# Per-token norm factor multiplied into the input once, ahead of the conditioning scale and shift, in a fused hybrid diffusion layer

## The chip, the cores and the metric

The kernel runs on one core of a Trainium2 chip. The metric is device time in microseconds for one execution of the whole layer, the median of several executions; smaller is better.

## The reference

One layer with a batch of 1, 1024 latent tokens of width 1024, and 256 context tokens. The part that the change touches is the first normalisation; cut to it:

```python
mod = (silu(c) @ ada_w + ada_b)          # 6 pieces: sh1, sc1, g1, sh2, sc2, g2
h  = rms_norm(x,   norm1_w) * (1 + sc1)  + sh1
hc = rms_norm(ctx, norm1_w) * (1 + sc1c) + sh1c
p, pc = h @ w_in, hc @ w_in              # q, k, v, z, x, B, C, dt columns
attn  = neighbourhood_attention(rope(q), rope(k), v, context keys and values)
y_ssd = rms_norm(bidirectional_ssd(...) * silu(z))
x = x + g1 * (concat(attn, y_ssd) @ w_out)
x = x + g2 * conv_glu(rms_norm(x, norm2_w) * (1 + sc2) + sh2)
return rms_norm(x, final_norm_w)
```

`rms_norm(x, w)` is x times the inverse root mean square of its row, times w.

## The kernel before

Activations lie with features on the 128 partitions (eight tiles, `kt` 0 to 7) and tokens along the free dimension; the 1024 tokens are taken in two halves, x0 and x1, of 512. A matrix product is done in three products of high and low parts (`mm3`): `hh` and `hl` are the high and low parts of the normalised input, `wh` and `wl` those of a weight, and each `kt` takes hh·wh, hl·wh and hh·wl. `load_w` loads a weight block of 128 columns (`ws`), splits it on ACT (`wh`, L79) and DVE (`wl`, L80). One such block over all 1024 tokens is a "unit" (`fu_...`), 48 matmuls of 128x512 into one PSUM tile of the pool `mmp`, which has three tiles.

The start of the kernel is the norm. `stats` squares the input on ACT and adds on DVE (`sqa_x`, L152), then sums over partitions on PE (`stat_x`). `rstd_rows` makes the inverse norm, a diagonal `dg_x` of it on DVE, and by a matmul with ones (L105) a tile `rbt` in PSUM that holds each token's factor on all partitions; `rbt` is one of the three tiles of `mmp`, and both halves lie in it. `ada(b)` loads a block of `ada_w` (`adaw`), multiplies it with the conditioning (`adap`, 8 matmuls, shown as x16 in some rows), copies it (`adas`) and transposes it (`mp`), from which DVE makes two columns each of `mod` and `modc`. Blocks 4 to 7 hold the scales and 0 to 3 the shifts, so that two tiles `kt` need block 4+i and block i. Then `norm` runs for each half and `kt`: DVE multiplies input, scale and `rbt` into `ny` (L176), ACT adds the shift and rounds to `hh` (L177), DVE takes `hl` as the rest (L178).

Behind the norm come the units of the q, k projections: `fu_qk00`, `fu_qk01`, `fu_qk10`, `fu_qk11`, `fu_qk20` and on. Each pair of units is rotated on DVE: `rp1_00`, `rp1_01` read the first unit's PSUM tile (L297), `rp2_00`, `rp2_01` the second's (L298), and the tiles come free with these. `context` normalises the context tokens: squares `sq_c` on ACT, `sqa_c` adds on DVE, `stat_c` on PE. Between them stands the load of `crow` (L319), a row for the late conditioning, put through Silu on ACT (L320); its place `yz` overlaps memory that the norm's work tiles hold before. In ACT's list, in both kernels, this Silu and the load of its table stand between `sq_c5` and `sq_c6`, so that the last two squares, the splits of the next weights and all that needs them come behind it.

The instruction order of each engine is written at build time by a scheduler that simulates the program; each engine then runs its own list in that order and waits where an operand isn't ready. Tiles of a pool are reused when their last reader is done.

Of the kernel before, what the change touches and what calls it, by code (L numbers as in the profile page):

```python
# [10 lines left out]
FP = mybir.dt.float32  # L11
FR = mybir.dt.float32r
AF = mybir.ActivationFunctionType
OP = mybir.AluOpType
# [3 lines left out]
P = 128  # L18
T = 1024
TC = 256  # L20
KT = 8
# [15 lines left out]
def hymba(ctx: ExitStack, tc: tile.TileContext, A):  # L37
    nc = tc.nc
    act, dve, pool, pe, sp = nc.scalar, nc.vector, nc.gpsimd, nc.tensor, nc.sync
# [4 lines left out]
    def f32(ap):  # L44
        return ap.bitcast(FP)
# [6 lines left out]
    mod = const.tile([P, 48], FP, name="mod")  # L52
    modc = const.tile([P, 16], FP, name="modc")
    scl = const.tile([P, 3, KT], FP, name="scl")
# [20 lines left out]
    def load_w(src, nk, nf, name):  # L75
        n = nk * nf
        s, h, l = (w_tile(tag, f"{tag}_{name}") for tag in ("ws", "wh", "wl"))
        sp.dma_start(s[:, :n], src)
        split[0] = act.activation(h[:, :n], s[:, :n], AF.Copy).ins  # L79
        dve.tensor_tensor(l[:, :n], s[:, :n], f32(h[:, :n]), OP.subtract)  # L80
        pat = "p (k f) -> p k f"
        return h[:, :n].rearrange(pat, k=nk), l[:, :n].rearrange(pat, k=nk)
# [10 lines left out]
    def rstd_rows(ps_pool, wk, sums, n, tag, key, dtag, dg=None, rb=None):  # L93
        st = wk.tile([P, 8], FP, tag="r_st", name=f"rst_{key}")
        act.activation(st[:, :n], sums, AF.Sqrt, bias=epst, scale=1.0 / 1024)
        dve.reciprocal(st[:, :n], st[:, :n])
        if rb is None:
            rb = ps_pool.tile([P, n * P], FP, tag=tag, name=f"rb_{key}")
        if dg is None:
            dg = wk.tile([P, n, P], FP, tag=dtag, name=f"dg_{key}", bufs=1)  # L100
        dve.tensor_tensor(dg, ident[:, None, :].to_broadcast([P, n, P]),
                          st[:, :n][:, :, None].to_broadcast([P, n, P]), OP.mult)
        for t in range(0, n, 4):
            e = min(n, t + 4)
            pe.matmul(rb[:, t * P:e * P], ones, dg[:, t:e], start=True, stop=True)  # L105
        return rb
# [1 line left out]

    pa = ExitStack()
    hx = pa.enter_context(tc.tile_pool(name="hx", reuse_waits="tile", bufs=1))  # L110
    pc = ExitStack()
    hxc = pc.enter_context(tc.tile_pool(name="hxc", reuse_waits="tile", bufs=1))
    hh = hx.tile([P, KT, T], FR, name="hh")
    hl = hx.tile([P, KT, T], FR, name="hl")
    ch = hxc.tile([P, KT, TC], FR, name="ch")
    cl = hxc.tile([P, KT, TC], FR, name="cl")

    mmp = pa.enter_context(tc.tile_pool(name="mmp", reuse_waits="tile", bufs=3, space=PSUM))
    m1p = pa.enter_context(tc.tile_pool(name="m1p", reuse_waits="tile", bufs=2, space=PSUM))
    pre = {}  # L120

    with ExitStack() as p0:
        adap = p0.enter_context(tc.tile_pool(name="adap", reuse_waits="tile", bufs=4))
        xin = p0.enter_context(tc.tile_pool(name="xin", reuse_waits="tile", bufs=1))
        wk0 = p0.enter_context(tc.tile_pool(name="wk0", reuse_waits="tile", bufs=2))

        cc = wk0.tile([P, KT, 2], FP, name="cc", bufs=1)
        sc = hx.tile([P, KT, 32], FP, name="sc")
        sel = wk0.tile([P, 2], FP, name="sel", bufs=1)
        xt = xin.tile([P, KT, T], FP, name="xt")  # L130
        sp.dma_start(cc, A["cc"])
        xh = [xt[:, :, 512 * h:512 * h + 512] for h in range(2)]

        def load_x(h):
            for kt in range(0, KT, 2):
                sp.dma_start(xh[h][:, kt:kt + 2], A["xt"][:, kt:kt + 2, 512 * h:512 * h + 512])

        load_x(0)
        sp.dma_start(sel, A["sel"])
        sp.dma_start(vec, A["vec"])  # L140
        sp.dma_start(cst, A["cst"])
        dve.memset(sc, 0.0)
        act.activation(sc[:, :, 0:2], cc, AF.Silu)

        def stats(wk0, src, n, key):
            st = m1p.tile([P, 8], FP, tag="m1", name=f"stat_{key}")
            acc = wk0.tile([P, n * P], FP, tag=f"sqa{n}", name=f"sqa_{key}", bufs=1)
            for kt in range(KT):
                sq = acc if kt == 0 else wk0.tile([P, n * P], FP, tag=f"ny{n}", name=f"sq_{key}{kt}", bufs=n)
                act.activation(sq, src[:, kt], AF.Square)  # L150
                if kt:
                    dve.tensor_tensor(acc, acc, sq, OP.add)  # L152
            for t in range(n):
                pe.matmul(st[:, t:t + 1], acc[:, t * P:(t + 1) * P], ones1, start=True, stop=True)
            return st[:, :n]

        def ada(b):
            w = adap.tile([P, KT, 256], FP, tag="ada", name=f"adaw{b}")
            sp.dma_start(w, A["ada_w"][b])
            pr = m1p.tile([P, 256], FP, tag="m1", name=f"adap{b}")  # L160
            for kt in range(KT):
                j = kt % 4
                pe.matmul(pr[32 * j:32 * j + 32], sc[:, kt], w[:, kt], start=kt < 4, stop=kt >= 4,
                          skip_group_check=True)
            sb = wk0.tile([P, 256], FP, tag="adas", name=f"adas{b}")
            act.activation(sb, pr, AF.Copy)
            mp = m1p.tile([P, 2, 2], FP, tag="m1", name=f"mp{b}")
            for f in range(2):
                pe.matmul(mp[:, f], sb[:, f * P:(f + 1) * P], sel, start=True, stop=True)
            c0 = 2 * b  # L170
            for m_, col in ((mod, 0), (modc, 1)):
                dve.tensor_tensor(m_[:, c0:c0 + 2], mp[:, :, col], vec[:, V_AB + c0:V_AB + c0 + 2], OP.add)

        def norm(src, rb, a, b, oh, ol, kt, n, key):
            y = wk0.tile([P, n], FP, tag=f"ny{n // P}", name=f"ny_{key}{kt}", bufs=n // P)
            dve.scalar_tensor_tensor(y, src[:, kt], a, rb, OP.mult, OP.mult)  # L176
            act.activation(oh[:, kt], y, AF.Identity, bias=b)  # L177
            dve.scalar_tensor_tensor(ol[:, kt], y, b, f32(oh[:, kt]), OP.add, OP.subtract)  # L178

        rbt = mmp.tile([P, T], FP, tag="mm", name="rbt")  # L180
        rbx = [rbt[:, 512 * h:512 * h + 512] for h in range(2)]
        rstd_rows(mmp, wk0, stats(wk0, xh[0], 4, "x0"), 4, "mm", "x0", "sqa4", rb=rbx[0])
        for i in range(4):
            ada(4 + i)
            if i == 0:
                load_x(1)
            ada(i)
            if i < 3:
                pre[i] = load_w(A["wf"][8 + i], KT, P, f"qk0{i}")
            s2 = slice(2 * i, 2 * i + 2)  # L190
            for j, m_ in enumerate((mod, modc)):
                dve.scalar_tensor_tensor(scl[:, j, s2], m_[:, 8 + 2 * i:10 + 2 * i], 1.0,
                                         vec[:, V_N1 + 2 * i:V_N1 + 2 * i + 2], OP.add, OP.mult)
            for h in range(2):
                if i == 0 and h:
                    rstd_rows(mmp, wk0, stats(wk0, xh[1], 4, "x1"), 4, "mm", "x1", "sqa4", rb=rbx[1])
                for kt in (2 * i, 2 * i + 1):
                    c = slice(512 * h, 512 * h + 512)
                    norm(xh[h], rbx[h], scl[:, 0, kt:kt + 1], mod[:, kt:kt + 1], hh[:, :, c], hl[:, :, c], kt, 512, f"x{h}")

    hs = (hh, hl)
    cs = (ch, cl)
    dtr = hx.tile([P, 10, 16], FP, name="dtr")
# [38 lines left out]
    with ExitStack() as p1:  # L242
# [67 lines left out]
        for b in range(2):  # L310
# [12 lines left out]
            for cb in range(4):  # L323
                win = v_d[4 * cb:4 * cb + 4, :, fs].rearrange("g (i r c) f -> r c (g i) f", i=2, r=2)
                for r in range(2):
                    p0 = 64 * r + CB0[cb]
# [273 lines left out]
    for i in range(2):  # L600
        t = at.tile([P, 1024], FP, name=f"tabt{i}", bufs=1)
# [474 lines left out]
    for hf_ in range(2):  # L1076
        c = slice(512 * hf_, 512 * hf_ + 512)
# [156 lines left out]
```

## Time and profile before

| what | value |
|---|---|
| median of 3 runs | 1395.33 us (1395.41, 1390.05, 1395.33) |
| profiled execution | 1391.19 us, span 1389.4 us |
| PE busy | 1328.5 us, 96% |
| DVE busy | 855.1 us, 62% |
| ACT busy | 628.0 us, 45% |
| POOL busy | 308.0 us, 22% |
| mean granted TensorE clock | 0.989 |

PE is TensorE's matmuls, DVE is VectorE, ACT is ScalarE, POOL is GpSimd, and SP is the engine whose queue issues most loads. The span is the time from the first to the last instruction. An engine that is busy 96% of the span sets the time nearly everywhere; the profile's rows say where it doesn't.

### The profile page before, as it was taken

The numbers are of one execution on the slowest core, as the hardware profiler recorded it, in microseconds if no ns is written. First come the engines' busy times: TensorE is split into PE (matmuls) and PEld (weight loads), VectorE is DVE, ScalarE is ACT, GpSimd is POOL, SyncE is SP. The second block draws the span as 40 slices with busy tenths as digits, with TensorE's granted clock in tenths as the row PEclk, the third lists the DMA queues.
The fourth block names the chain that finished last, engine by engine and source line by source line (L and its number), as shares of the span: only waits on it lengthen the run. The fifth ranks groups of instructions, "written<-read, shape, count | busy, mean of one in ns | idle before, by whom it ended". The sixth has DMA issues, their size and how long they took to land.

```text
span 1389.4 us, 20030 instructions
## 1 busy us (share of the span) xinstructions
PE 1328.5 (96%) x7539; PEld 1116.4 (80%) x7539; DVE 855.1 (62%) x1343; ACT 628.0 (45%) x1052; POOL 308.0 (22%) x297
## 2 busy tenths in 40 slices
PE   5999999999989999999999999999999999999996
PEld 3788998889968877777887888888888878888884
DVE  5683347652367766647887555666556586585663
ACT  5441224342155557536556444454445464364440
POOL 0000000013667862000222222221222111201210
PEclk9999999999999999999999999999999999999998
DMA  9565575621697697333858576766677796777771
GB/s 370 212 159 139 142 231 198 220 92 38 164 269 213 206 241 250 124 114 121 205 121 212 153 185 163 175 153 157 144 174 169 204 289 184 169 214 210 182 187 71
DMA packets 118160, 251.02 MB, mean 181 GB/s; under 512 B 11944, under 2 KB 37288, under 8 KB 116784
## 3 DMA queue, kind: packets, MB, share of 16 engines
q1 hardware_dynamic: 92576, 197.58, 44.4%
q0 software_dynamic: 25488, 52.18, 20.2%
q8 instruction: 59, 0.97, 0.3%
q14 instruction: 37, 0.30, 0.1%
HBM read 212.16 MB, written 37.55 MB: 180 GB/s over the span
## 4 chain that ended last, share of the span: by engine, by line
PE 79%; DMA 8%; DVE 4%; ACT 4%; issue 2%; POOL 1%; SPq 0%; DVEq 0%; POOLq 0%; ACTq 0%
PE u L872 28%; PE fu_qk L90 7%; PE fu_x L90 6%; PE pd L90 6%; PE tu_v L90 4%; PE tu_z L90 3%; PE oc L90 3%; PE av L666 3%; PE pm L1044 2%; PE pt L648 2%; PE os L90 2%; PE s L627 1%; PE oa L90 1%; PE fu_c L90 1%; DMA g_d<-xa 1%
## 5 line engine op out<-in xcount | busy, mean ns | idle before, releaser
L872 PE MATMUL u<-op,whu 128*128 128x512 f32 (+1 forms) x760 | 225.9, 380 | 2.3 <-DVE op L827 0.9
L872 PEld LDWEIGHTS u<-op,whu 128*128 128x128 f32 x760 | 138.9, 188 | 33.3 <-DVE op L827 1.1
L864 ACT ACTIVATE whu<-as 128x512 fp32r<-128x512 f32 x115 | 67.8, 627 | 175.3 <-PE u L872 167.0
L845 POOL DMA_DIRECT2D as<-in_w_up x69 | 66.4, 985 | 360.0 <-DMA as<-in_w_up 153.2
L872 PE MATMUL u<-op,wlu 128*128 128x512 f32 (+1 forms) x380 | 143.4, 378 | 0.0
L872 PE MATMUL u<-opx,whu 128*128 128x512 f32 (+1 forms) x384 | 110.0, 377 | 1.6 <-ACT whu L864 1.2
L865 DVE TENSOR_TENSOR wlu<-as,whu 128x512 fp32r<-128x512 f32 x115 | 76.0, 686 | 25.3 <-ACT whu L864 25.1
L872 PEld LDWEIGHTS u<-opx,whu 128*128 128x128 f32 x384 | 69.8, 188 | 17.2 <-ACT whu L864 2.3
L872 PEld LDWEIGHTS u<-op,wlu 128*128 128x128 f32 x380 | 71.3, 188 | 14.9
L90 PE MATMUL pd<-opx,wh_dn 128*128 128x512 f32 x256 | 81.7, 402 | 0.5 <-ACT wh_dn L79 0.3
L895 DVE TENSOR_TENSOR xa<-u,yz 128x512 f32<-128x512 f32 (+1 forms) x24 | 15.5, 646 | 99.2 <-PE u L872 99.2
L872 PE MATMUL u<-opx,wlu 128*128 128x512 f32 (+1 forms) x192 | 71.7, 376 | 0.0
L639 ACT ACTIVATE pr<-pr,mx 128x640 f32<-128x640 f32 x64 | 52.9, 827 | 39.1 <-DVE mx L638 39.0
L638 DVE CUSTOM_DVE_ANT_0 pr<-s,tabt 128x640 f32<-128x640 f32 x64 | 52.0, 818 | 20.0 <-PE s L628 15.9
L666 PE MATMUL av<-pts,vp 128*64 128x128 f32 x640 | 55.3, 284 | 5.7 <-ACT pts L650 5.2
L852 POOL DMA_DIRECT2D yz<-in_w_up x46 | 55.0, 1230 | 22.8 <-ACT yz L851 21.9
L90 PEld LDWEIGHTS pd<-opx,wh_dn 128*128 128x128 f32 x256 | 47.8, 189 | 12.6 <-ACT wh_dn L79 1.1
L650 ACT ACTIVATE pts<-pt 128x640 f32<-128x640 f32 x64 | 43.9, 696 | 30.3 <-PE pt L648 19.8
L872 PE MATMUL u<-opz,whu 128*128 128x512 f32 (+1 forms) x192 | 56.3, 376 | 0.4 <-ACT yz L887 0.4
L648 PE MATMUL pt<-cst,pr 128*128 128x128 f32 x320 | 48.5, 282 | 6.9 <-ACT pr L639 3.4
L666 PEld LDWEIGHTS av<-pts,vp 128*64 128x64 f32 x640 | 40.5, 139 | 18.2 <-ACT pts L650 8.4
L90 PE MATMUL pd<-opx,wl_dn 128*128 128x512 f32 x128 | 51.2, 402 | 1.6 <-DVE wl_dn L80 1.6
(643 smaller groups left out, 3573.3 us busy)
## 6 DMA issues: line engine op xcount, KB each, us to landing
as<-in_w_up SPq DMA_DIRECT2D x69, 256.0 KB, 4.0
as<-in_w_up POOLq DMA_DIRECT2D x69, 256.0 KB, 3.8
yz<-in_ada_wt SPq DMA_DIRECT2D x32, 512.0 KB, 4.7
ws_dn<-in_w_down SPq DMA_DIRECT2D x32, 448.0 KB, 4.0
as<-in_w_up SPq DMA_DIRECT2D x23, 512.0 KB, 5.5
yz<-in_w_up POOLq DMA_DIRECT2D x46, 256.0 KB, 5.8
g_d<-xa POOLq DMA_DIRECT2D x22, 512.0 KB, 5.0
tabt<-in_tab SPq DMA_DIRECT2D x48, 192.0 KB, 4.4
```

The lines of the kernel that those rows point to most:

```text
L90: pe.matmul(out[:, t0:t1], st(a, k), mv(b, k, t0, t1), start=k == 0 and p == 0, stop=k == kend - 1 and p == 2, **kw)
L638: dve.tensor_tensor_reduce(pr, ps[:, lo:lo + 640], tabt[m % 2][:, 384 * j:384 * j + 640], -1.0, BIG, OP.add, OP.min, mx)
L639: act.activation(pr, pr, AF.Exp, bias=mx, scale=-1.0, accum_out=sm[:, n % 8:n % 8 + 1])
L648: pe.transpose(pt[:, i * P:(i + 1) * P], pr[:, i * P:(i + 1) * P], ident)
L650: act.activation(pts, pt[:, 0:640], AF.Copy)
L666: pe.matmul(av[64 * j:64 * j + 64, cb], vt, pp[j][:, i * P:(i + 1) * P], start=i == 0, stop=i == 4, skip_group_check=True)
L845: pool.dma_start(t, d, accum_op=OP.add)
L852: pool.dma_start(t, d, accum_op=OP.add)
L864: act.activation(h, src, AF.Copy)
L865: dve.tensor_tensor(l, src, f32(h), OP.subtract)
L872: mm = pe.matmul(ps[:, t0:t1], aops[n, o][a][:, k], bops[o][b][:, k, t0:t1], start=first and o < 5 and (t0 == 0 or n == 2), stop=end, skip ...
L1044: pe.matmul(dst[o], aops[n, o][a][:, k], sops[o][b][:, k], start=k == i == 0 and (o in (0, 2, 4) or o > 4 and first), stop=k == 3 and i == ...
```

## The change

The product with `rbt` is taken out of `norm` and done for all eight tiles of a half right after that half's `rbt` (`unit`, in place in the input `xt`). `norm` then has ACT make `hh` from the input with the scale and the shift, ACT take the shift from it again (`nt`, a new tile, with the negated shift `neg`), and DVE make `hl` as input times scale minus `nt`. The pool of `adaw` has six buffers instead of four, and the context's tiles `ch` and `cl` are opened after the norm's pools are closed.

```diff
@@ -108,19 +108,15 @@
 
     pa = ExitStack()
     hx = pa.enter_context(tc.tile_pool(name="hx", reuse_waits="tile", bufs=1))
-    pc = ExitStack()
-    hxc = pc.enter_context(tc.tile_pool(name="hxc", reuse_waits="tile", bufs=1))
     hh = hx.tile([P, KT, T], FR, name="hh")
     hl = hx.tile([P, KT, T], FR, name="hl")
-    ch = hxc.tile([P, KT, TC], FR, name="ch")
-    cl = hxc.tile([P, KT, TC], FR, name="cl")
 
     mmp = pa.enter_context(tc.tile_pool(name="mmp", reuse_waits="tile", bufs=3, space=PSUM))
     m1p = pa.enter_context(tc.tile_pool(name="m1p", reuse_waits="tile", bufs=2, space=PSUM))
     pre = {}
 
     with ExitStack() as p0:
-        adap = p0.enter_context(tc.tile_pool(name="adap", reuse_waits="tile", bufs=4))
+        adap = p0.enter_context(tc.tile_pool(name="adap", reuse_waits="tile", bufs=6))
         xin = p0.enter_context(tc.tile_pool(name="xin", reuse_waits="tile", bufs=1))
         wk0 = p0.enter_context(tc.tile_pool(name="wk0", reuse_waits="tile", bufs=2))
 
@@ -171,15 +167,22 @@
             for m_, col in ((mod, 0), (modc, 1)):
                 dve.tensor_tensor(m_[:, c0:c0 + 2], mp[:, :, col], vec[:, V_AB + c0:V_AB + c0 + 2], OP.add)
 
-        def norm(src, rb, a, b, oh, ol, kt, n, key):
-            y = wk0.tile([P, n], FP, tag=f"ny{n // P}", name=f"ny_{key}{kt}", bufs=n // P)
-            dve.scalar_tensor_tensor(y, src[:, kt], a, rb, OP.mult, OP.mult)
-            act.activation(oh[:, kt], y, AF.Identity, bias=b)
-            dve.scalar_tensor_tensor(ol[:, kt], y, b, f32(oh[:, kt]), OP.add, OP.subtract)
+        neg = wk0.tile([P, KT], FP, name="neg", bufs=1)
+
+        def unit(src, rb):
+            for kt in range(KT):
+                dve.tensor_tensor(src[:, kt], src[:, kt], rb, OP.mult)
+
+        def norm(y, a, b, nb, oh, ol, kt, key):
+            t = wk0.tile([P, 512], FP, tag="nt", name=f"nt_{key}{kt}", bufs=4)
+            act.activation(oh[:, kt], y[:, kt], AF.Identity, scale=a, bias=b)
+            act.activation(t, f32(oh[:, kt]), AF.Identity, bias=nb)
+            dve.scalar_tensor_tensor(ol[:, kt], y[:, kt], a, t, OP.mult, OP.subtract)
 
         rbt = mmp.tile([P, T], FP, tag="mm", name="rbt")
         rbx = [rbt[:, 512 * h:512 * h + 512] for h in range(2)]
         rstd_rows(mmp, wk0, stats(wk0, xh[0], 4, "x0"), 4, "mm", "x0", "sqa4", rb=rbx[0])
+        unit(xh[0], rbx[0])
         for i in range(4):
             ada(4 + i)
             if i == 0:
@@ -191,13 +194,19 @@
             for j, m_ in enumerate((mod, modc)):
                 dve.scalar_tensor_tensor(scl[:, j, s2], m_[:, 8 + 2 * i:10 + 2 * i], 1.0,
                                          vec[:, V_N1 + 2 * i:V_N1 + 2 * i + 2], OP.add, OP.mult)
+            dve.tensor_scalar(neg[:, s2], mod[:, s2], -1.0, None, OP.mult)
             for h in range(2):
                 if i == 0 and h:
                     rstd_rows(mmp, wk0, stats(wk0, xh[1], 4, "x1"), 4, "mm", "x1", "sqa4", rb=rbx[1])
+                    unit(xh[1], rbx[1])
                 for kt in (2 * i, 2 * i + 1):
                     c = slice(512 * h, 512 * h + 512)
-                    norm(xh[h], rbx[h], scl[:, 0, kt:kt + 1], mod[:, kt:kt + 1], hh[:, :, c], hl[:, :, c], kt, 512, f"x{h}")
-
+                    norm(xh[h], scl[:, 0, kt:kt + 1], mod[:, kt:kt + 1], neg[:, kt:kt + 1], hh[:, :, c], hl[:, :, c], kt, f"x{h}")
+
+    pc = ExitStack()
+    hxc = pc.enter_context(tc.tile_pool(name="hxc", reuse_waits="tile", bufs=1))
+    ch = hxc.tile([P, KT, TC], FR, name="ch")
+    cl = hxc.tile([P, KT, TC], FR, name="cl")
     hs = (hh, hl)
     cs = (ch, cl)
     dtr = hx.tile([P, 10, 16], FP, name="dtr")
```

The first place is the start of DVE's list, behind `dg_x0`, the diagonal of the first half's factors; `xt` is the input, `sqa_x1` the sum of squares of the second half. Before:

```order
L101 TENSOR_TENSOR dg_x0_152<-cst_61,rst_x0_149 128x512
L172 TENSOR_TENSOR mod_65<-mp4_168,vec_60 128x2
L172 TENSOR_TENSOR modc_66<-mp4_168,vec_60 128x2
L192 SCALAR_TENSOR_TENSOR scl_67<-mod_65,vec_60 128x2
L192 SCALAR_TENSOR_TENSOR scl_67<-modc_66,vec_60 128x2
L176 SCALAR_TENSOR_TENSOR ny_x00_203<-xt_109,scl_67,rbt_120 128x512
L176 SCALAR_TENSOR_TENSOR ny_x01_207<-xt_109,scl_67,rbt_120 128x512
L152 TENSOR_TENSOR sqa_x1_212<-sqa_x1_212,sq_x11_214 128x512
```

After:

```order
L101 TENSOR_TENSOR dg_x0_148<-cst_61,rst_x0_145 128x512
L174 TENSOR_TENSOR xt_104<-xt_104,rbt_116 128x512 x8
L168 TENSOR_TENSOR mod_65<-mp4_172,vec_60 128x2
L168 TENSOR_TENSOR modc_66<-mp4_172,vec_60 128x2
L148 TENSOR_TENSOR sqa_x1_217<-sqa_x1_217,sq_x11_219 128x512
L195 SCALAR_TENSOR_TENSOR scl_67<-mod_65,vec_60 128x2
L195 SCALAR_TENSOR_TENSOR scl_67<-modc_66,vec_60 128x2
L148 TENSOR_TENSOR sqa_x1_217<-sqa_x1_217,sq_x12_222 128x512
```

Eight products stand ahead of the second half's sums, where two stood, and the later `ny` are gone from the list.

The second place is PE's list just behind the second half's `rbt`, where the first units begin; numbers behind the names are the program's own. Before:

```order
L90 MATMUL fu_qk00_448<-hh_87,wh_qk00_196 128x512
L90 MATMUL fu_qk00_448<-hl_88,wh_qk00_196 128x512
L90 MATMUL fu_qk01_497<-hh_87,wh_qk01_290 128x512
L90 MATMUL fu_qk01_497<-hl_88,wh_qk01_290 128x512
L169 MATMUL mp1_284<-sel_108,adas1_282 128x2 x2
L163 MATMUL adap6_315<-adaw6_313,sc_107 32x256 x8
L90 MATMUL fu_qk00_448<-hl_88,wh_qk00_196 128x512
```

After:

```order
L90 MATMUL fu_qk00_469<-hh_84,wh_qk00_200 128x512
L90 MATMUL fu_qk00_469<-hl_85,wh_qk00_200 128x512
L90 MATMUL fu_qk01_518<-hh_84,wh_qk01_303 128x512
L90 MATMUL fu_qk01_518<-hl_85,wh_qk01_303 128x512
L165 MATMUL mp1_297<-sel_103,adas1_295 128x2 x2
L90 MATMUL fu_qk10_590<-hh_84,wh_qk02_364 128x512 x2
L90 MATMUL fu_qk10_590<-hl_85,wh_qk02_364 128x512
L159 MATMUL adap6_329<-adaw6_327,sc_102 32x256 x8
```

The third unit, `fu_qk10`, which before began behind `mp3_404`, some 55 rows further on, begins here; its PSUM tile is the one that `rbt` held, and it waits for the last product of `unit(x1)`.

The third place is the end of the first three units on PE, and on DVE the rotation that frees their tiles. PE before:

```order
L90 MATMUL fu_qk10_569<-hh_87,wh_qk02_350 128x512 x2
L90 MATMUL fu_qk10_569<-hl_88,wh_qk02_350 128x512 x2
L90 MATMUL fu_qk10_569<-hh_87,wl_qk02_351 128x512 x2
L90 MATMUL fu_qk11_624<-hh_87,wh_qk11_619 128x512 x2
L90 MATMUL fu_qk11_624<-hl_88,wh_qk11_619 128x512 x2
L154 MATMUL stat_c_696<-ones1_63,sqa_c_697 128x1
L90 MATMUL fu_qk11_624<-hh_87,wl_qk11_620 128x512 x2
```

PE after:

```order
L90 MATMUL fu_qk10_590<-hl_85,wh_qk02_364 128x512
L90 MATMUL fu_qk10_590<-hh_84,wl_qk02_365 128x512 x2
L90 MATMUL fu_qk11_645<-hh_84,wh_qk11_640 128x512 x2
L90 MATMUL fu_qk11_645<-hl_85,wh_qk11_640 128x512 x2
L150 MATMUL stat_c_717<-ones1_63,sqa_c_718 128x1 x2
L90 MATMUL fu_qk20_789<-hh_84,wh_qk20_784 128x512 x2
L90 MATMUL fu_qk20_789<-hl_85,wh_qk20_784 128x512 x2
L90 MATMUL fu_qk11_645<-hh_84,wl_qk11_641 128x512 x2
```

On PE all three units now end together, and behind them stand `fu_qk11` and `fu_qk20`, four matmuls each, ahead of the first use of `wl_qk11`. DVE before:

```order
L152 TENSOR_TENSOR sqa_c_697<-sqa_c_697,sq_c5_711 128x256
L152 TENSOR_TENSOR sqa_c_697<-sqa_c_697,sq_c6_714 128x256
L152 TENSOR_TENSOR sqa_c_697<-sqa_c_697,sq_c7_717 128x256
L297 SCALAR_TENSOR_TENSOR rp1_00_547<-fu_qk00_448,cossin_443 128x1024
L297 SCALAR_TENSOR_TENSOR rp1_01_551<-fu_qk00_448,cossin_443 128x1024
L80 TENSOR_TENSOR wl_qk11_620<-ws_qk11_618,wh_qk11_619 128x1024
```

DVE after:

```order
L148 TENSOR_TENSOR sqa_c_718<-sqa_c_718,sq_c5_732 128x256
L148 TENSOR_TENSOR sqa_c_718<-sqa_c_718,sq_c6_735 128x256
L306 SCALAR_TENSOR_TENSOR rp1_00_568<-fu_qk00_469,cossin_464 128x1024
L306 SCALAR_TENSOR_TENSOR rp1_01_572<-fu_qk00_469,cossin_464 128x1024
L148 TENSOR_TENSOR sqa_c_718<-sqa_c_718,sq_c7_738 128x256
L307 SCALAR_TENSOR_TENSOR rp2_00_569<-fu_qk01_518,cossin_464 128x1024
L307 SCALAR_TENSOR_TENSOR rp2_01_573<-fu_qk01_518,cossin_464 128x1024
L80 TENSOR_TENSOR wl_qk11_641<-ws_qk11_639,wh_qk11_640 128x1024
```

On DVE the first two rotations now stand ahead of the last `sqa_c`, and all four ahead of `wl_qk11`. `fu_qk11` takes the PSUM tile that `rp1_01` frees, `fu_qk20` the one that `rp2_01` frees.

## Rows read from the trace of the kernel before

**Rows 1.** Page: head, busy time by engine, GB/s in 40 slices.

```profile
span 1389.4 us, 20030 instructions
...
PE 1328.5 (96%) x7539; PEld 1116.4 (80%) x7539; DVE 855.1 (62%) x1343; ACT 628.0 (45%) x1052; POOL 308.0 (22%) x297
...
GB/s 370 212 159 139 142 231 198 220 92 38 164 269 213 206 241 250 124 114 121 205 121 212 153 185 163 175 153 157 144 174 169 204 289 184 169 214 210 182 187 71
```

**Rows 2.** Timeline of PE, 10 to 39 us: start, length, instruction, idle before.

```profile
15.34 2.08 PE L105 MATMUL rbt<-dg_x,cst 128*128 128x512 f32 x2
...
26.50 1.84 PE L154 MATMUL stat_x<-ones,sqa_x 128*128 128x1 f32 x8 [0.15 <-DVE sqa_x L152]
```

**Rows 3.** Timeline of DVE, 10 to 39 us.

```profile
18.49 1.41 DVE L176 SCALAR_TENSOR_TENSOR ny_x<-xt,scl,rbt 128x512 f32<-128x512 f32 x2
19.81 4.67 DVE L152 TENSOR_TENSOR sqa_x<-sqa_x,sq_x 128x512 f32<-128x512 f32 x6
24.53 1.23 DVE L80 TENSOR_TENSOR wl_qk<-ws_qk,wh_qk 128x1024 fp32r<-128x1024 f32 x1
25.67 0.68 DVE L152 TENSOR_TENSOR sqa_x<-sqa_x,sq_x 128x512 f32<-128x512 f32 x1
```

**Rows 4.** Chain that ended last, 30 to 80 us: start, length, what.

```profile
30.93 1.71 PE rbt L105 x2
...
37.56 1.00 PE adap L163 x16
38.56 4.38 PE fu_qk L90 x18
...
59.19 17.72 PE fu_qk L90 x76
```

**Rows 5.** Timeline of ACT, 55 to 90 us.

```profile
59.42 2.57 ACT L177 ACTIVATE hh<-ny_x,mod 128x512 fp32r<-128x512 f32 x4 [4.43 <-DVE mod L172]
...
67.17 1.28 ACT L320 ACT_TABLE_LOAD   x1 [2.40 <-DMA yz<-in_crow]
```

**Rows 6.** Timeline of DVE, 55 to 90 us.

```profile
60.18 2.75 DVE L178 SCALAR_TENSOR_TENSOR hl<-ny_x,mod,hh 128x512 fp32r<-128x512 f32 x4 [0.73 <-ACT hh L177]
...
69.87 0.96 DVE L152 TENSOR_TENSOR sqa_c<-sqa_c,sq_c 128x256 f32<-128x256 f32 x2 [4.49 <-ACT sq_c L150]
70.74 2.35 DVE L297 SCALAR_TENSOR_TENSOR rp<-fu_qk,cossin 128x1024 f32<-128x1024 f32 x2
73.00 1.22 DVE L80 TENSOR_TENSOR wl_qk<-ws_qk,wh_qk 128x1024 fp32r<-128x1024 f32 x1
```

**Rows 7.** Timeline of SP, 55 to 90 us: the issue of the loads.

```profile
62.99 0.33 SPq L319 DMA_DIRECT2D yz<-in_crow  x1
```

**Rows 8.** Waits of SP's queue, 55 to 75 us: total, times, longest.

```profile
SPq L319 <- DVE hl L178: 8.1, 1, 8.1
```

**Rows 9.** Five stretches: busy PE, PEld, DVE, ACT, POOL; clock, DMA share, GB/s.

```profile
100.00:350.00 250.00, 250.00 (x1575) 225.65 (x1574) 116.74 (x171) 77.50 (x109) 27.34 (x25) 1.00 0.50 152
350.00:560.00 210.00, 193.56 (x1542) 167.65 (x1540) 136.40 (x240) 112.06 (x214) 128.30 (x88) 0.97 0.78 224
490.00:498.00 8.00, 8.00 (x46) 7.09 (x45) 3.41 (x6) 3.86 (x8) 4.40 (x3) 0.57 0.96 206
1100.00:1250.00 150.00, 143.54 (x764) 121.18 (x763) 113.66 (x215) 80.67 (x156) 18.80 (x22) 0.99 0.77 217
1206.00:1212.00 6.00, 5.93 (x29) 5.43 (x30) 5.12 (x9) 3.23 (x6) 1.43 (x2) 0.72 0.76 148
```

**Rows 10.** Timeline of PE, 484 to 492 us.

```profile
489.23 0.43 PE L666 MATMUL av<-pts,vp 128*64 128x128 f32 x2 [2.72 <-ACT pts L650]
```

**Rows 11.** Timeline of PE, 1200 to 1210 us.

```profile
1206.07 0.50 PE L1044 MATMUL pm<-op,whu('d', 0, 2)2_10050 128*128 128x256 f32 x2 [2.08 <-ACT yz L1052]
```

**Rows 12.** Chain that ended last, 370 to 390 us.

```profile
373.60 0.61 ACT zs L570
...
380.66 4.27 DMA tabt<-in_tab
```

## The prediction

> **What bounds the kernel now.** I read the page first: PE is busy 1328.5 of 1389.4 us [rows 1], so the time is PE's work plus the places where PE waits. An edit to DVE and ACT alone counts where it makes PE wait, or stops it from waiting. Next the chain that ended last: behind the second half's `rbt` it is PE alone, 18 matmuls in 4.38 us and so on up to 76 in 17.72 us from 59.19 [rows 4], 0.233 us each, with no wait. So whatever delays PE's start with the second half's factors comes out at the far end of the units, and is not made good in between. Then the timelines of DVE, ACT and SP around the norm. They show what lies just under PE: the last `hl` ends at 60.18 + 2.75 = 62.93 and the load of `crow`, which had waited 8.1 us for it, is issued at 62.99 [rows 6 to 8]. ACT then stands 2.40 us for that load and starts the table at 67.17 [rows 5], DVE gets its last `sqa_c` at 69.87 after 4.49 us of idling, and the two rotations that free a PSUM tile end at 70.74 + 2.35 = 73.09 [rows 6]. PE needs this tile at 59.19 + 72 x 0.233 = 75.98 (the 76 of that row less the four of the fourth unit). The slack is 2.9 us.
>
> **The change, step by step.** Starting at one state for both kernels, I follow the delay.
>
> (1) *Work.* 16 `ny` become 16 unit products, 16 `hl` stay, 4 tiny `neg` come. ACT gets 16 `nt` beside 16 `hh`. Neither engine is the bound (62% and 45%), so this is free where other work covers it; what counts is order.
>
> (2) *First half.* `rbt` x0 ends at 15.34 + 2.08 = 17.42 [rows 2]. An `ny`, one PSUM and one SBUF operand of 128x512, takes 0.70 us (1.41 for two), an add of two SBUF tiles 0.68 to 0.69 [rows 3]. I take 0.70 for a unit product: eight take 5.6 us and end at 23.05, where the two `ny` ended at 19.90. The seven adds, `wl` (1.23 [rows 3]) and the small ones behind them follow; the last add ends near 30.15 against 25.67 + 0.68 = 26.35 before: **+3.8**. The nearest lower bound is half of that price, as for an operation that took two elements a cycle; no row shows such a one on DVE here.
>
> (3) *Second half.* From the start of `stat_x` to the end of `rbt` x1 PE and DVE need 30.93 + 1.71 - 26.50 = 6.14 us [rows 2, 4]; with the delay that ends near 36.35. In the old order PE went on with the blocks of the conditioning and the first two units while two `ny` were made. In the new one the third unit stands there, six matmuls into the first two; its PSUM tile is that of `rbt`, so it waits for all eight products: 36.35 + 5.6 and the start of an instruction, **42.1**. Before, PE was at the same matmul at 38.56, and had one block of `adap` more behind it (1.00 us at 37.56 [rows 4]); so PE is 42.1 + 1.0 - 38.56 = **4.5** late here. I don't see that the work that PE finds meanwhile (a block, six matmuls) shortens it, since it is in both.
>
> (4) *The three units.* Until their end 138 matmuls, 4 blocks and 4 small `mp` follow: 138 x 0.233 + 4.0 + 1.4 = 37.6, with 0.6 for the wait for the last `hl` behind `mp3`, so 80.3 against 75.98: **+4.3**, as it should be from step 3.
>
> (5) *The last shift.* `mp3` now has two thirds of the third unit ahead of it. It ends at 42.1 + 90 x 0.233 + 4.0 + 1.4 = 68.45 against 59.19: +9.3. Behind it `hh` takes 2.57 us for four [rows 5], then four `nt` at the same pitch of 0.64, and `hl`, at 2.75 for four [rows 6], can follow them one by one: the last `hl` ends 6.2 us behind `mp3` (3.74 before) at 74.7. `crow` goes with it. From its issue to the end of the two rotations it was 73.09 - 62.99 = 10.1 us [rows 6, 7], less the 0.4 of the last add, which now stands behind the rotations: PE gets the tile of the fourth unit at **84.4**. It ran dry at 80.3. So the slack of 2.9 us has become a wait of **4.1**: 2.9 are eaten by the delay of `mp3`, `nt` and the rest that PE's own delay doesn't cover. An estimate with the Trainium skill, ScalarE: Activation LUTs, What ACT_TABLE_LOAD costs, goes 0.4 us further: it adds 93 ns for each pointer operand of an ACTIVATE, and the new `hh` has two where L177 has one. No row here shows that pair in this size, and the sum leaves it out.
>
> (6) *Behind it.* Four matmuls on, the fifth unit waits for the other pair of rotations, 84.4 + 0.4 + 2.35 = 87.15, and the next matmul of the fourth for `wl_qk11`, 1.22 us [rows 6] later, **88.35**. PE will by then have done 8 matmuls and `stat_c` of the next work (2.0 us), which before stood at 77.97. So PE is 10.4 late: 4.3 of step 4, 4.1 of step 5, 2.0 here.
>
> (7) *The clock.* The trace shows what PE pays after idling: 2.72 us without a matmul [rows 10], then a mean granted clock of 0.57 over 8 us, which is 0.43 x 8 = 3.4 us of work lost; after 2.08 us [rows 11] it is 0.72 over 6 us, 1.7 lost [rows 9]. That is the lower level of 1.2 GHz for part of these stretches. By the Trainium skill, TensorE: Matmul & The Clock Gate, Part 1, this lower level is the resting state that activity lifts, so that every pause that is long enough costs, that of step 3 too; the rows agree for the two pauses that they show, and by the rule the sum would be up to 1.7 higher, 14.6. Two waits of 4.1 and 2 us with one us of work between them should cost as much again: I take **2.5**, between the two. At step 3 the idle is 1 to 3 us and I take nothing, with 1.7 as its upper bound.
>
> (8) *The rest.* Six buffers let two blocks of `ada_w` overtake the third weight block, 2.1 MB or 5.7 us at the 370 GB/s of the first slice [rows 1]; that weight is needed only at 42.1, so it costs nothing. Its loads end well before that as far as the rate tells (some 12 MB in all by then, 33 us); if the units could start 9 us sooner, it would begin to count. `ch` and `cl` are written long after, by `context`. From 100 to 350 us PE is busy 250.00 of 250.00 [rows 9], in one order in both kernels. At 373.60 the next wait of PE hangs on `zs`, which ACT makes of PE's last result, and the table loads that end the wait are issued behind that (4.27 us from 380.66 [rows 12]). So it moves along with PE and gives nothing back.
>
> The sum is 10.4 + 2.5 = **+12.9**, made against the profiled execution: 1391.2 + 12.9 = 1404.1. That execution lies 4.1 below the median, as one of three runs does; on the median's basis it is 1408.2. I say **1406**, between them. Bounds: with products at half price the second half is ready while PE still works; what then stays is the place of the third unit ahead of `mp3` (24 matmuls, 5.6 us), the `nt` and the dry end: mp3 near 63.9, last `hl` 70.1, fourth unit 79.8, step 6 at 83.7, or +5.7, 1397 to 1401. Upwards the clock of both waits at 3.4 and 1.7 gives +15.5, 1407 to 1411.
>
> **Rivals.**
>
> *A. The attention stage takes it up (not slower).* Over 350 to 560 us PE is busy 193.56 of 210 [rows 9]: 16.4 us of idling with DMA at 0.78, and at 0.96 in 490 to 498. If loads there were the limit and went out at a time that PE doesn't set, the whole 12.9 would vanish: 1391 to 1396. It decides at the table loads: it needs them issued before PE's last `tu_z`. Against it: [rows 12] has their issue behind `zs`. 0.12.
>
> *B. The products are cheap, or run in gaps.* +5.7 as above, 1397 to 1401, mostly within 0.5%. It decides where eight products take under some 2.8 us. The two rows nearest to it are both at 0.7. 0.10.
>
> *C. The reordered down projection gains.* PE's list differs again there, and over 1100 to 1250 us PE idles 6.5 us [rows 9]. If the new order filled these, 12.9 - 6.5 = +6.4: 1397.5 to 1402. The work is the same and its releasers (a weight split, a copy from ACT) aren't touched, so it could as well lose some. 0.12.
>
> *D. The dry end costs more.* If PE stays at the lower level through both waits, or the load of `crow` meets the late blocks, add 3 to 6: 1409 to 1414. 0.08.
>
> *E. The change removes a wait that I don't see* in PE's first 38 us, by earlier blocks of `ada_w`, and is faster, below 1388. For it: PE idles most there. Against it: what ends it is DVE's sums, which come later. 0.05.
>
> The forecast itself holds 0.53, from 1401 to 1410. 0.5%, 7 us, is about what a measurement of this kernel can tell from no change; its three runs spread by 5.4. Slower by more than that: most of the forecast, all of D, a little of C: 0.60. Within it: A in the main, B, C and the lower part of the forecast: 0.32. Faster: E and the edge of A, 0.08. The range of 8 in 10 takes in B, C and most of D: 1394 to 1412. The forecast's own range is 1401 to 1410.
>
> **What would show it.** In the changed kernel's trace: eight products of 0.70 each and the last add near 30; PE standing until 42 for the third unit; `mp3` near 68.5 and the last `hl` near 74.7; the load of `crow` issued right behind; PE idle near 80.3 to 84.4 with DVE's rotations as the releaser, a second wait to 88.4, and a clock below 1 behind them; then the same spacing as before from 90 to 370. I would be wrong if the crow load came out ahead of the last `hl`, if the third unit didn't wait for the eighth product, or if the attention stage began less late than the q, k units ended.

## The result, and the profile after

The changed kernel takes 1407.26 us (median of 4 runs, 1405.49 to 1413.87) against 1395.37 beside it; the ratio is 1.0097, 95% interval [1.0069, 1.0124]. The profiled execution took 1407.97 us. It is slower, by about the forecast amount. The page's head and busy times, to be read beside [rows 1]:

```profile
span 1406.2 us, 20046 instructions
...
PE 1332.6 (95%) x7539; PEld 1117.4 (79%) x7539; DVE 857.0 (61%) x1347; ACT 637.5 (45%) x1068; POOL 312.7 (22%) x297
```

PE has 4 us more of busy time and 17 us more of span: it waits, and works at the lower clock. The timeline of DVE at the start, as [rows 3] (start, length, instruction, idle before):

```profile
17.60 4.87 DVE L174 TENSOR_TENSOR xt<-xt,rbt 128x512 f32<-128x512 f32 x8 [2.61 <-PE rbt L105]
...
28.11 0.69 DVE L148 TENSOR_TENSOR sqa_x<-sqa_x,sq_x 128x512 f32<-128x512 f32 x1
...
35.12 4.87 DVE L174 TENSOR_TENSOR xt<-xt,rbt 128x512 f32<-128x512 f32 x8 [1.83 <-PE rbt L105]
39.91 0.15 DVE L168 TENSOR_TENSOR mod<-mp,vec 128x2 f32<-128x2 f32 x1
```

Eight products take 4.87 us, 0.61 each and not the 0.70 of the forecast. The last sum of the second half ends at 28.80 (26.35 before, 30.15 forecast). The second eight end at 39.99, and behind them stand `mod` and `modc` of the next block. PE's timeline there:

```profile
38.91 0.61 PE L165 MATMUL mp<-sel,adas 128*128 128x2 f32 x4 [1.00 <-ACT adas L162]
40.14 0.70 PE L90 MATMUL fu_qk<-hh,wh_qk 128*128 128x512 f32 x2 [0.62 <-DVE modc L168]
```

PE starts the third unit at 40.14 (42.1 forecast). Its list waits there for the eighth product, which ended 0.15 us before; the trace names `modc`, the last to end on DVE. Two pieces of the chain that ended last (start, length, what), the second half's `rbt` and `mp3`:

```profile
33.38 1.72 PE rbt L105 x2
...
67.13 0.35 PE mp L165 x4
```

`mp3` is done at 67.48 (68.45 forecast, 59.19 before [rows 4]). Then ACT, DVE and SP, as [rows 5 to 7]:

```profile
67.70 2.94 ACT L178 ACTIVATE hh<-xt,mod,scl 128x512 fp32r<-128x512 f32 x4 [5.22 <-DVE mod L168]
70.54 2.55 ACT L179 ACTIVATE nt_x<-hh,neg 128x512 f32<-128x512 f32 x4
...
78.46 1.28 ACT L329 ACT_TABLE_LOAD   x1 [1.71 <-DMA yz<-in_crow]
```

```profile
71.28 2.74 DVE L180 SCALAR_TENSOR_TENSOR hl<-xt,scl,nt_x 128x512 fp32r<-128x512 f32 x4 [3.41 <-ACT nt_x L179]
...
81.50 2.35 DVE L306 SCALAR_TENSOR_TENSOR rp<-fu_qk,cossin 128x1024 f32<-128x1024 f32 x2
...
86.36 3.49 DVE L80 TENSOR_TENSOR wl_qk<-ws_qk,wh_qk 128x1024 fp32r<-128x1024 f32 x3
```

```profile
74.09 0.33 SPq L328 DMA_DIRECT2D yz<-in_crow  x1
```

The last `hl` ends at 74.02, `crow` is issued at 74.09, ACT stands 1.71 us for it, and the two rotations end at 83.85. PE's timeline at that place, and six stretches of 2 us (busy time of PE, PEld, DVE, ACT, POOL; clock, DMA share, GB/s):

```profile
79.34 0.62 PE L90 MATMUL fu_qk<-hh,wl_qk 128*128 128x512 f32 x2
83.99 1.19 PE L90 MATMUL fu_qk<-hh,wh_qk 128*128 128x512 f32 x2 [4.03 <-DVE rp L306]
...
86.59 1.19 PE L90 MATMUL fu_qk<-hh,wh_qk 128*128 128x512 f32 x2
...
90.06 0.62 PE L90 MATMUL fu_qk<-hl,wh_qk 128*128 128x512 f32 x2
```

```profile
80.00:82.00 2.00, 0.00 (x0) 0.00 (x0) 0.85 (x2) 2.00 (x4) 0.00 (x0) 1.00 0.68 279
82.00:84.00 2.00, 0.01 (x1) 0.04 (x1) 2.00 (x3) 2.00 (x3) 0.00 (x0) 0.78 0.00 0
84.00:86.00 2.00, 2.00 (x6) 1.61 (x6) 2.00 (x3) 1.55 (x2) 0.00 (x0) 0.50 0.00 0
86.00:88.00 2.00, 2.00 (x8) 1.72 (x7) 2.00 (x3) 0.26 (x1) 0.00 (x0) 0.50 0.03 8
88.00:90.00 2.00, 2.00 (x6) 1.60 (x5) 2.00 (x3) 0.00 (x0) 0.00 (x0) 0.51 0.72 213
90.00:92.00 2.00, 2.00 (x10) 1.60 (x10) 2.00 (x3) 0.98 (x2) 0.00 (x0) 1.00 0.97 279
```

PE runs dry at 83.99 - 4.03 = 79.96 (80.3 forecast) and goes on at 83.99 (84.4). Behind this the granted clock is 0.50, 1.2 GHz, until 90. The second wait of the forecast does not appear: at the lower clock the eight matmuls and `stat_c` last so long that the second pair of rotations is done when PE comes to `fu_qk20` at 86.59, and `wl_qk11` soon enough too. I call the wait from 79.96 to 83.99 the dry end below.

To follow the lag through the program I counted PE's 7539 matmuls and set the start of the same number in two traces side by side. Behind the units PE's lists are the same in before and after, but for numbers 4404 to 4452 (near 720 us), until 6225; from there to 6892, in the down projection (1135 to 1262 us), they differ in pieces. The table also has the experiments below; a lag is the time by which a kernel is behind the first execution of before.

```
lag to the kernel before, us, at the start of matmul number
                                  300    2000    6200    6500    7500
before (start, us)              70.26  349.60 1128.89 1184.51 1368.95
before, second execution        -1.27   -1.27   +0.67   +0.79   +1.01
changed                         +3.96  +11.04  +11.95  +16.09  +16.64
changed, second execution       +4.38  +11.79  +11.78  +16.10  +16.81
four buffers                    +4.05   +5.82  +12.64  +14.66  +17.00
third unit late                 +4.05   +4.24   +9.05   +9.51  +11.26
crow late                       +4.07   +7.97  +10.80  +10.54  +13.45
third unit and crow late        +3.07   +3.12   +7.38   +5.70   +5.79
second half's products twice    +6.20  +12.71  +17.52  +18.43  +18.41
split only                      +2.18   +2.26   +4.33   +8.47  +13.98
products held                   -1.78   -1.74   -4.47   -5.00   -1.76
products held, again            -0.48   -0.44   +0.70   +1.10   +4.99
products held, four buffers     +7.11   +7.14  +18.95  +23.45  +23.96
```

So 11.0 of the 16.8 us between the two spans arise in the first 92 us, stay to 0.05 us until the attention stage (10.99 at matmul 400), and 4.7 more arise in the down projection. Between them, from 2000 to 6200, lie the attention stage and what follows it, where executions of one kernel drift apart by up to 4 us (the two of the held products). Most experiments lose 2 to 5 us there, the two with four buffers 6.8 and 11.8; why was not looked into. The traces of four buffers, third unit late, split only and held with four buffers are of the slowest execution of their kernel, so their last columns lie above their medians, and the head, up to 2000, is the safest comparison.

### The profile page after: what moved, and what is told of

Read it like the earlier page. It is cut to its first block, busy times and chain, and to the rows that moved or that the text cites. A ratio compares the mean times of both kernels' runs of the same rounds, so it can differ in the third digit from the quotient of the medians.

```text
span 1406.2 us, 20046 instructions
## 1 busy us (share of the span) xinstructions
PE 1332.6 (95%) x7539; PEld 1117.4 (79%) x7539; DVE 857.0 (61%) x1347; ACT 637.5 (45%) x1068; POOL 312.7 (22%) x297
## 4 chain that ended last, share of the span: by engine, by line
PE 71%; DMA 11%; DVE 7%; ACT 4%; issue 3%; POOL 3%; SPq 0%; DVEq 0%; POOLq 0%; ACTq 0%
PE u L881 27%; PE fu_x L90 6%; PE fu_qk L90 6%; PE pd L90 5%; PE tu_v L90 4%; PE oc L90 3%; PE tu_z L90 2%; PE av L675 2%; PE os L90 2%; PE pt L657 2%; DMA seg<-cum_d 2%; PE oa L90 1%; PE fu_c L90 1%; PE s L636 1%; DMA as('d', 1, 2)1_11212<-in_w_down 1%
```

## The experiments

My theory was the forecast's: the place of the products delays PE's start, draws the third unit ahead of `mp3`, so that `crow` and with it ACT's and DVE's queues come late, and PE runs dry. The rivals were the longer split over ACT, the buffers and loads, and a delay that later stages take up. Each ratio is to runs of before on the same chip.

**Controls.** Both kernels again, unchanged.

> The kernel before, unchanged, in a second profiled execution. It tells apart what of the 16.8 us between the two spans (1406.2 and 1389.4) belongs to the change. Theory: the first 360 us repeat to 0.2 us (the 2000th matmul at 349.6), and the 4 to 6 us of difference that arise past 1140 us, in the down projection, are partly the execution's own spread, since the medians differ by 11.9 only: the 7500th matmul at 1369 to 1374. Rival: the reordered down projection costs 5 us in every execution; then it repeats at 1369 within 1 us.

> The changed kernel, unchanged, in a second profiled execution, for the 5 us that it loses past 1140 us in the down projection. Theory from the control of before (whose lag stayed within 1 us there): the reordered list costs 3 to 6 us there in every execution, so the lag between the 6200th and the 7500th matmul grows by 3 to 6 us again. Rival (an accident of one execution): by less than 1.5 us. The first 360 us: 11 us behind within 1.5 us.

Before: 1392.32 us, ratio 0.9982 [0.9964, 0.9999], so the comparison itself can be off by 0.2%. Its head came 1.27 us sooner, where I had expected a repeat within 0.2. Changed: 1409.24, ratio 1.0112 [1.0085, 1.0139]. Its loss in the down projection came again (11.78 to 16.81), before's lag grew by 0.3 there: the theory for it held, an accident is out. PE's waits in the changed kernel's first execution from 1137 us on (engine, line, releaser: total, times, longest):

```profile
PE pd L90 <- DVE wl_dn L80: 2.7, 5, 0.9
PE pd L90 <- ACT op L964: 2.3, 1, 2.3
...
PE pd L90 <- ACT wh_dn L79: 1.5, 3, 0.8
```

These three come to 6.5 us (8.5 in its second execution); the same releasers gave 3.7 in before (1.8, 1.6 and 0.3). They are splits of `w_down` and a copy, in the same code but in another order. That this order costs is shown by the other kernels: two more have the changed kernel's order there, split only and held with four buffers, and the rest have before's. From 6200 to 6500 the four executions with the new order lose 4.1 to 4.5 us, the eight with the old one -1.7 to +2.0. Which move in it does was not tried. From 6500 to 7500 the two groups overlap: 0.5 to 5.5 us and 0 to 3.9.

**Four buffers.**

```diff
-        adap = ...tile_pool(name="adap", reuse_waits="tile", bufs=6)
+        adap = ...tile_pool(name="adap", reuse_waits="tile", bufs=4)
```

> The changed kernel with four buffers for the conditioning blocks instead of six. The prediction's step 8 says that the buffers cost nothing: then the 2000th matmul stays 11 us behind that of before and the time at about 1407. Rival: the two more buffers push the work tiles of the norm onto the place of crow, so that crow's load waits for the last hl; with four its load and its Silu stand in the middle of the norm, the dry end of PE (4.0 us) and the half clock behind it (3.4 us) go, and the 2000th matmul is 3 to 6 us behind: 1399 to 1402.

1400.97 us, ratio 1.0035 [1.0010, 1.0060], and a lag of 5.82 instead of 11.04 at matmul 2000. The rival held, and step 8 fell in that part. In the down projection this kernel has before's order, so its time lacks that loss too. ACT's timeline in this kernel:

```profile
33.00 1.28 ACT L329 ACT_TABLE_LOAD   x1
34.29 1.06 ACT L329 ACTIVATE yz<-yz 128x1024 f32<-128x1024 f32 x1
```

Table and Silu of `crow` stand at 33.0, not behind the last `hl`: the load no longer waits for the norm's tiles. In before, with four buffers too, it does wait for the last `hl` [rows 8], so what frees the place is four buffers together with the late `ch` and `cl`; by the sizes in the code these two take as much as two buffers. PE still waits for the rotations, but 1.1 us instead of 4.0.

**Third unit late.** Its matmuls queued on PE behind `mp3`.

```diff
+            mp3[0] = mpi.ins
 ...
+                with tc.issue_after(mp3[0]) if (blk, f2) == (1, 0) else nullcontext():
                     pq.append(fm_unit(wt, hs, T, mmp, "mm", f"qk{blk}{f2}"))
```

> The changed kernel with the third unit queued on PE behind mp3, as before, so that it no longer waits early for the eighth product nor delays mp3. Theory: mp3 and with it the last hl and crow come some 7 us sooner (mp3 near 61 to 62), the dry end of 4.0 us and its half clock go; what stays is the start of the first two units 2 to 4 us late. 2000th matmul 3 to 5 us behind before, time 1399 to 1401. Rival (the loss is the longer chain hh, nt, hl or the early loads): the dry end stays, 9 to 11 us behind, 1405 to 1407.

1397.43 us, ratio 1.0020 [1.0002, 1.0038], lag 4.24. The theory held, though `mp3` came 4.3 us sooner and not 7, and the time is below its range; its chain:

```profile
36.27 1.73 DVE xt L176 x3
...
38.66 1.28 DVE xt L176 x2
39.95 0.07 DVE mod L170
40.02 0.08 DVE modc L170
...
40.13 1.07 PE adap L160 x16
41.21 5.94 PE fu_qk L90 x18
...
62.87 0.34 PE mp L166 x4
63.21 16.83 PE fu_qk L90 x72
```

From 63.21 there are 72 matmuls without a gap and the dry end is gone. What stays is the start: PE's block at 40.13 follows DVE's products, since the `mod` and `modc` that it waits for are queued behind them. That is 2.6 us of the 4.24 (40.13 for 37.56 [rows 4]). The other 1.6 are the clock: the 18 matmuls behind the block take 5.94 us and not 4.38 [rows 4], with a granted clock of 0.50 from 42 to 44 us. PE had stood 1.00 and 0.67 us before it; in the changed kernel it stood 1.00 and 0.62 there, and the clock stayed at 1.00.

**Crow late.** Only its Silu, behind the context's split on ACT.

```diff
+                split_c[0] = act.activation(ch[:, kt], y, AF.Copy).ins
 ...
-                act.activation(crow, crow, AF.Silu)
+                with tc.issue_after(split_c[0]):
+                    act.activation(crow, crow, AF.Silu)
```

> The changed kernel with only the Silu of crow queued on ACT behind the split of the context, so that squares and weight splits no longer stand behind crow's load. Theory: PE still ends the three units near 80, but the tile of the fourth unit comes free near 80.3 instead of 83.9; then a wait near 1 us for the other rotations and a short one for wl_qk11, no half clock: 2000th matmul 5 to 8 us behind before, time 1401 to 1404. Rival (the dry end is due to DVE's rotations alone, not to crow): 10 to 11 us behind, 1406 to 1407.

1402.85 us, ratio 1.0056 [1.0036, 1.0077], lag 7.97. PE's timeline:

```profile
81.23 0.70 PE L90 MATMUL fu_qk<-hh,wh_qk 128*128 128x512 f32 x2 [0.81 <-ACT wh_qk L79]
...
83.49 0.90 PE L90 MATMUL fu_qk<-hh,wh_qk 128*128 128x512 f32 x2 [1.10 <-DVE rp L309]
```

The wait of 4.03 is now 0.81 and 1.10, and the second half of the forecast's mechanism is shown apart from the first. Against my expectation the clock fell here too (the matmul pairs from 84.19 take 1.05 in place of 0.62), after 1.9 us of idling in two pieces.

**Both.** The two edits together.

> The changed kernel with both the third unit behind mp3 and crow's Silu behind the context's split. Theory: the dry end is gone with the third unit's place alone, so the Silu's place adds nothing: 2000th matmul 3.5 to 5 us behind before, as with the third unit alone (4.2), time 1396 to 1399. Rival (crow still holds something up): 2 to 3 us less, 1394 to 1396.

1397.11 us, ratio 1.0016 [0.9997, 1.0034], lag 3.12, a little under my 3.5 to 5. The 1.1 us to the third unit alone are less than that kernel's 1.6 of lower clock, which this trace doesn't have there (1.00 from 40 to 46 us): the Silu's place adds nothing once the third unit is late.

**Products held.** Each product made just ahead of its block, and on DVE behind an earlier block's `hl`; split on ACT, six buffers and late `ch`, `cl` as in the change.

```diff
-        def norm(y, a, b, nb, oh, ol, kt, key):
+        def norm(y, rb, a, b, nb, oh, ol, kt, key):
+            with tc.issue_after(low[0]) if low[0] else nullcontext():
+                dve.tensor_tensor(y[:, kt], y[:, kt], rb, OP.mult)
 ...
-        unit(xh[0], rbx[0])
 ...
-                    unit(xh[1], rbx[1])
```

> The changed kernel with each product held on DVE to its own block, in the place that the ny had, everything else as changed (split on ACT, six buffers, late ch and cl). The tile of rbt then comes free late again and the third unit moves behind mp3 of its own accord. Theory: all of the 11 us in the first 100 us hang on where the products stand; the longer chain through nt (2.5 us) fits into the slack of 2.9 us ahead of the rotations. 2000th matmul 0 to 1.5 us behind before, time 1394 to 1398. Rival (the split on ACT or the six buffers cost by themselves): 3 us behind or more, 1398 to 1403.

> The kernel of the held products once more, unchanged, timed more often, because its first time (1391.0, ratio 0.9987) lies below before by less than the interval. Theory: its q, k units start 1.5 to 2 us sooner, since the second half's sums stand two small products earlier, and the lag stays: ratio 0.997 to 0.9995, 2000th matmul 1 to 2.5 us ahead of before. Rival (one execution's spread): ratio 1.000 within 0.001.

1391.04 us, ratio 0.9987 [0.9966, 1.0008], and 1395.04, ratio 0.9991 [0.9971, 1.0012]; lags -1.74 and -0.44. All of the loss is gone with the place of the products alone: in the head, and in the down projection, whose list is before's again. PE's waits up to 120 us in the first of the two:

```profile
PE stat_x L150 <- DVE sqa_x L148: 11.7, 1, 11.7
PE adap L159 <- DMA adaw<-in_ada_w: 2.9, 1, 2.9
PE mp L165 <- ACT adas L162: 0.6, 1, 0.6
```

No wait for a unit's operand or tile is left. The head is not slower than before, and better than the 0 to 1.5 that I expected. That it is faster isn't shown: before's own second execution has -1.27, and the repeat's -0.44 missed the 1 to 2.5 us of its theory.

**Split only.** Before's `ny` kept, and the low part taken over `nt`.

```diff
-            dve.scalar_tensor_tensor(ol[:, kt], y, b, f32(oh[:, kt]), OP.add, OP.subtract)
 ...
+            act.activation(t, f32(oh[:, kt]), AF.Identity, bias=nb)
+            dve.tensor_tensor(ol[:, kt], y, t, OP.subtract)
```

> The kernel before, with ny kept on DVE (input times scale times factor), and only the low part taken over the new tile nt from ACT: 16 ACTIVATEs more and nothing else. Theory: the last hl ends 2.5 us later, within the slack of 2.9 us; 2000th matmul 0 to 1 us behind, time within 0.3% of before. Rival (the slack is smaller than read, or ACT delays the weight splits): a dry end of 1 to 3 us, 1397 to 1400.

1403.02 us, ratio 1.0066 [1.0048, 1.0083]. In the head the theory came close: no dry end, lag 2.26 where I had expected up to 1. The time was a miss: 9.7 us arose between matmuls 6200 and 7500, in a stage that the edit doesn't touch. 4.1 of them, up to 6500, go with the changed kernel's order, which this list has there; the other 5.5 stand in the slowest of eight executions. So the low cost of the split is shown by the head, not by this time.

**Products of the second half twice.**

> The changed kernel with the eight products of the second half done twice, so that its factor is applied twice (the values of that half differ): a dose of 4.9 us of DVE work at the place in question. Theory: PE starts the third unit 4.9 us later and nothing behind gives it back: 2000th matmul 15 to 17 us behind before, time 1411 to 1413. Rival (PE is held by something else than the eighth product, or the end of the units by a fixed time of crow): less than 2 us more than the changed kernel's 11, 1407 to 1409.

1410.50 us, ratio 1.0118 [1.0082, 1.0153]; lag 12.71, 1 to 1.7 more than the changed kernel's two executions. The rival's lag came and its time didn't (1407 to 1409), but the timeline of PE shows why the lag is small:

```profile
39.23 1.07 PE L159 MATMUL adap<-adaw,sc 128*32 128x256 f32 x16 [2.65 <-DVE modc L168]
...
43.82 1.94 PE L159 MATMUL adap<-adaw,sc 128*32 128x256 f32 x16
45.68 1.22 PE L90 MATMUL fu_qk<-hh,wh_qk 128*128 128x512 f32 x2
```

The third unit starts at 45.68, 5.5 us later, as expected. But the scheduler put two more blocks of the conditioning ahead of it, which otherwise stand between units, so most of the dose was filled. The dose does not tell the theories apart.

**Products held, with four buffers.**

> Held products with four buffers, so that crow is loaded and put through Silu in the middle of the norm. Theory: with the third unit late PE never ran dry there, so crow's early load gains nothing: 2000th matmul within 1 us of the six-buffer version, ratio to before 0.996 to 1.000. Rival (the early load and table switch take ACT's time in the norm, where PE waits for it): 1 to 4 us slower, 1393 to 1396.

1404.83 us, ratio 1.0066 [1.0044, 1.0087], lag 7.14: the rival held in its direction, at over twice its size. ACT's timeline:

```profile
32.40 1.28 ACT L330 ACT_TABLE_LOAD   x1
33.70 1.06 ACT L330 ACTIVATE yz<-yz 128x1024 f32<-128x1024 f32 x1
34.70 1.52 ACT L178 ACTIVATE hh<-xt,mod,scl 128x512 fp32r<-128x512 f32 x2
```

Table and Silu stand ahead of an `hh` that PE waits for, and PE waits 3.3 us for `hh` and `hl` in the norm; behind these waits the granted clock is 0.50 twice (38 to 40 and 62 to 64 us). What part of the 8.9 us between this kernel and the six-buffer one is theirs, and what part the later blocks', was not separated. So four buffers help the changed kernel and harm this one; that the early `crow` does the harm is the likely reading, and not shown.

## Why the prediction was right, point by point

**Steps 2 and 3, the late start**, held with a smaller size. A product is 0.61 and not 0.70, so PE was at the third unit at 40.14, 40.14 + 1.0 - 38.56 = 2.6 late and not 4.5. Of the difference 1.35 us stand in the first half's sums (28.80 for 30.15): its eight products ended 2.57 late (22.47 for 19.90), the last sum 2.45, and the 0.65 that the forecast added on the way from 3.15 to 3.8, without a working, did not come. The rest is the second eight. I had put the wait on the unit's PSUM tile alone. With the unit moved away the same 2.6 stay, because the next block waits at the same time for `modc`, queued behind the products: the queue, not the tile, makes the start late.

**Step 4** gave 4.3; it was 79.96 - 75.98 = 4.0. Two errors cancel: a start 2.0 us too late, and a pitch of 0.233 us taken from an unbroken stretch, where matmuls between blocks take 0.243 (18 in 4.38 [rows 4]); the waits for `hl` came as assumed (0.7 for 0.6). By the same matmul number the lag is 2.7 at 290 and 3.96 at 300, behind these waits.

**Step 5, the dry end**, was forecast as 4.1 and is 4.03, and the experiments show its cause on both sides: it goes when the third unit moves behind `mp3`, and shrinks when `crow`'s Silu moves or when `crow`'s place is freed. The groups of the two new operations in the changed kernel, and below them those of `ny` and `hh` in before (count, busy time, mean):

```profile
L178 ACT ACTIVATE hh<-xt,mod,scl 128x512 fp32r<-128x512 f32 x16 | 11.8, 805 | 13.7 <-DVE mod L168 10.7 <-DVE xt L174 2.7 <-DVE scl L195 0.3
...
L174 DVE TENSOR_TENSOR xt<-xt,rbt 128x512 f32<-128x512 f32 x16 | 9.7, 681 | 4.4 <-PE rbt L105 4.4
```

```profile
L176 DVE SCALAR_TENSOR_TENSOR ny_x<-xt,scl,rbt 128x512 f32<-128x512 f32 x16 | 11.0, 743 | 0.0
L177 ACT ACTIVATE hh<-ny_x,mod 128x512 fp32r<-128x512 f32 x16 | 10.5, 714 | 11.9 <-DVE mod L172 10.9 <-DVE ny_x L176 1.0
```

`hh` with scale and shift means 805 ns, where `hh` with the shift alone meant 714 in before; four take 2.94 us, not 2.57. That is the estimate by the Trainium skill, ScalarE: Activation LUTs, What ACT_TABLE_LOAD costs, of 93 ns for a pointer: the trace agrees with 91, and 0.37 us of step 5 were missing in the sum.

**Steps 6 and 7** failed as a sum. I added 2.0 for a second wait and 2.5 for the clock; together they were 11.04 - 3.98 - 4.03 = 3.0. They lie in one another: at the lower clock PE takes as long for eight matmuls as the rotations need. The clock by itself, 0.50 from 84 to 90, is 3 us of work. The nothing that I took for the clock at step 3 held in the changed kernel (1.00 from 40 to 46 us), but not as a rule: at that place the traces of third unit late and four buffers have 0.50 from 42 to 44 us, 1.6 us of work in the first, close to the bound of 1.7.

**Step 8** failed twice. The buffers are not free: with four, 5.2 of the 11 us go, because two more of them lay the norm's tiles over the place of `crow`. Against before they take nothing, since its load waits for the last `hl` there too; they take back what the late `ch` and `cl` had opened. I had looked at their loads, and not at what their memory displaces. And the down projection, rival C, gained nothing but lost 4.7 to 5.0 us, in both executions, 4.1 to 4.3 of them where its list differs. Rivals A and B are out: the lag stays at 11 through the attention stage's start, and ends within 1 us of it at 755 us and beyond; products below 2.8 us for eight did not come.

The total of 12.9 stands against 16.8 between the profiled executions, 11.9 between the medians first measured and 15.7 with the second set. That the point, 1406, was so near is in part luck: a head that was forecast 1.9 us too long and a down projection missing by 4.7 met a basis put between two.

## What to carry to other kernels

Work that is the same in amount can cost by where it stands in a queue: eight products in a row put what stands behind them 2.5 us later (the sums at 28.80 for 26.35, PE's block at 40.13 for 37.56 where the third unit is out of the way), and freed a PSUM tile that drew a later unit forward, which in turn delayed the last shift and all that hung on it. Before a tile is freed earlier, ask what will take it, and what that stands ahead of. More buffers should be priced by the memory that they push aside as well as by the waits that they remove; and a local edit under a scheduler is judged by its own stage in the trace, since the reordered down projection cost 4 us by itself, and its executions differ by as much again.

## What the runs showed of the hardware

An in-place product of 128x512 with a PSUM operand means 681 ns, where the same with a scale besides (`ny`) meant 743 in before; back to back they take 0.61 and 0.70 us. And the granted clock that the profile shows in the first 40 us is not to be relied on: in the second execution of before it reads 0.52 from 20 to 34 us,

```profile
20.00:34.00 14.00, 10.84 (x63) 6.51 (x67) 10.59 (x20) 8.85 (x14) 0.00 (x0) 0.52 1.00 408
34.00:38.00 4.00, 4.00 (x37) 2.60 (x30) 4.00 (x10) 1.44 (x4) 0.00 (x0) 0.99 1.02 414
```

while the first reads 1.00 there,

```profile
20.00:34.00 14.00, 10.44 (x59) 6.32 (x63) 10.59 (x17) 8.58 (x14) 0.00 (x0) 1.00 1.00 407
```

yet in both a block of `adap` takes 1.93 us near 28 us and 1.07 past 36. In the trace of third unit and crow late it reads 1.00 from 36 to 40 us, where matmuls at 38.4 to 39.2 us start 0.43 apart, as they do at 0.50 in the changed kernel from 84.5 us on. The matmuls' own durations are the better sign there. And the clock is not the same in every execution: PE stood 1.00 us and 0.5 to 0.7 us at the same place near 40 us in the traces of the changed kernel, four buffers and third unit late, and the clock fell behind it in the last two and not in the first.
